# Gated recurrence of a two-layer trunk: half of the tokens reversed, one product per level over packed keys, the diagonal by a product with ones

## Chip, cores and metric

The kernel runs on one core of a Trainium2 chip. The metric is the device time of one execution in microseconds. Before the change it is 628.70 us, the median of three runs (628.10 to 628.72). The engines are called as in the profile: PE is TensorE, DVE is VectorE, ACT is ScalarE, POOL is GpSimd, SP issues most DMAs.

## What is computed

A trunk of two layers over 256 tokens of 1024 features in float32. Layer 0 mixes tokens by a gated linear recurrence with 8 heads of 128 features, layer 1 by causal attention with a table of relative positions. A feed-forward part follows each.

```python
def hgrn2_mixer(h, w_in, w_out, lb, out_norm):
    # S_t = diag(f_t) S_{t-1} + (1 - f_t) i_t^T ; o_t = S_t^T q_t, per head
    q, fz, inp, og = jnp.split(h @ w_in, ...)
    q = silu(q)
    f = lbf + (1.0 - lbf) * sigmoid(fz)
    k = 1.0 - f
    ...
    o = rms_norm(o, out_norm) * sigmoid(og)
    return o @ w_out

def reference(x, ...):
    for layer in range(2):
        y = rms_norm(h, norm_mix[layer])
        y = hgrn2_mixer(y, ...) if layer == 0 else moba_mixer(y, ...)
        h = h + y
        h = h + swiglu(rms_norm(h, norm_ffn[layer]), ...)
    return rms_norm(h, final_norm)
```

In closed form, the score of query t on key s (s not after t) is the sum over the 128 features n of q[t,n] k[s,n] f[s+1,n] ... f[t,n], and the output is the sum of scores times the input i.

## The kernel before

**The stream of products.** Each weight is split into a rounded part and a rest, whi and wlo, both in a rounded 32-bit format, and each activation into xh and xl (hh and hl in the feed-forward part). A weight tile of 128 x 128 is used in three *main products* with 256 columns: whi with xh, wlo with xh, whi with xl (`mm_w`, all issued in L478). The weights come as blocks of 128 x 1024 by DMA from SP into `raw`; ACT writes whi (L435), DVE writes wlo (L437). The ring of whi and wlo holds six blocks, and a new whi waits until PE has done with the block six places earlier.

**The recurrence of a head** works on q and k with features on the partitions and the 256 tokens along the free axis, as two halves of 128 tokens. The products of the gates are taken by levels m = 1, 2, 4, ..., 64. At level m the tokens lie in pairs of blocks of m, and queries of the late block meet keys of the early block; the weights between them are products of gates. `forget` (L815) makes f, k and, on POOL, the gate products tot of blocks of 2, 4, ..., 64 (L831). `query` (L834) makes q. `step` (L858) goes from level m to 2m: it multiplies half of q and half of k by tot on DVE (L865, L867) and copies the other halves on ACT (L869, L872) into new tiles Q[2m], K[2m].

`scores` (L896) issues the products. The first (L919, tile mov) has 192 columns for each half: the diagonal, which uses k and silu(q) before any gate, and level 1. The levels 2, 4, 8, 16 (L913) have 64 columns for each half, so two products a level. Level 32 and level 64 share two products of 128 columns (L940), because ACT has joined them (L879, L881), and the *far* product of half 1's queries on half 0's keys has 128 (L942). All these operands are float32. DVE copies what a mask admits from PSUM into the score tile pm (L907, L924), ACT copies level 32, 64 and far (L950 to L954). Two value products of pm with ii follow (L961, L962), then `result` (L966) makes the next split activations.

**Order.** The class `Order` decides it while the program is built: each operation has an engine, a cost, a due time and the buffers it waits for. Between main products the scheduler places what it takes for ready by its costs; products of the recurrence are placed 1.5 us (by its clock) after their operands are ready. Each engine then runs its queue strictly in that order. The projections of two heads (`EARLY_HEADS`) run at the opening together with the token-wide projection; six heads follow, three projections of 24 main products each, and then the output projection w_out with 192 main products, in which the norm over all heads (sto: sums, power on POOL, transposes L621, row rrow on ACT) is finished. `residual` (L626) multiplies by that row on DVE (yt), adds (hT) and makes the xh (ACT, L565) and xl (DVE) of the first feed-forward layer.

**The table** of attention (L1010 to L1026): a product of 384 columns (L1019), one DMA to DRAM and eight DMAs back from POOL that skew it into bt. The logits read it in L1162.

Of the kernel before, what the change touches and what calls it, by code (L numbers as in the profile page):

```python
# [15 lines left out]
P = 128  # L16
S = 256
# [12 lines left out]
LEVELS = (1, 2, 4, 8, 16)  # L30
# [295 lines left out]
def hybrid_trunk(ctx: ExitStack, tc: tile.TileContext, wts, xT, par, gfin, tab, onehot, masks, out):  # L326
# [14 lines left out]

    def new(tag, shape, bufs=1, dt=FT, held=False):
        return ring(tag, shape, bufs, dt).new(held)
# [204 lines left out]
    bt = new("bt", [P, NH * S])  # L548
    bt.tile = bt.ring.make()
    mk = fixed("mk", [P, NMK], U8)  # L550
    oh = fixed("oh", [33, 384])
# [3 lines left out]
    def tables():  # L555
        od.op("S", 60, lambda: nc.sync.dma_start(mk.tile, masks), writes=[mk], nbytes=NMK * P, due=65)
        od.op("S", 60, lambda: nc.sync.dma_start(oh.tile, onehot), writes=[oh], nbytes=60000, due=100)
# [244 lines left out]

    class Core:
# [3 lines left out]
        def __init__(self, h):  # L807
            self.h = h
            self.f = new("ff", [P, S], 2)
            self.so = new("so", [P, S], 3)  # L810
            self.Q = {m: new(f"q{m}", [P, S], 2) for m in (1, 2, 4, 8, 16, 32, 64)}
            self.K = {m: new(f"k{m}", [P, S], 2) for m in (1, 2, 4, 8, 16, 32, 64)}
            self.tot = {1: self.f}

        def forget(self, b):  # L815
# [6 lines left out]
            k1 = self.K[1]  # L822
            od.op("A", ca(S), lambda: A.activation(k1.tile, f.tile, AF.Identity, scale=-1.0, bias=1.0), reads=[f],
                  alloc=[k1], due=7)
            for m in (1, 2, 4, 8, 16, 32):
# [6 lines left out]
                od.op("G", cg(S // (2 * m)), prod, reads=[a], alloc=[t], due=8)  # L832

        def query(self, b):  # L834
            f, q1 = self.f, self.Q[1]
            b, src = normed(self.h, b, 6)
            sg = new("sgq", [P, S], 3)
            self.mov = mov = new("mov", [P, 2, 192], 2)
            two = lambda t: t.rearrange("p (a t) -> p a t", a=2)
            od.op("A", ca(S), lambda: A.activation(sg.tile, src(), AF.Sigmoid), reads=[b], alloc=[sg], due=6)  # L840
            od.op("V", cv(S), lambda: V.tensor_tensor(mov[:, :, :P], two(src()), two(sg.tile), op=OP.mult),
                  reads=[b, sg], alloc=[mov], due=6)
            od.op("V", cv(S), lambda: V.tensor_tensor(two(q1.tile), mov[:, :, :P], two(f.tile), op=OP.mult),
                  reads=[mov, f], alloc=[q1], due=7)
            od.op("A", ca(P), lambda: A.activation(
                mov[:, :, P:], q1.tile.rearrange("p (a t z) -> p a t z", a=2, z=2)[:, :, :, 1], AF.Copy),
                reads=[q1], writes=[mov], due=8)
# [10 lines left out]
        def step(self, m, due):  # L858
            Q, K, tot = self.Q, self.K, self.tot[m]
            nb = S // (2 * m)  # L860
            if m < 64:
                q, qn, k, kn = Q[m], Q[2 * m], K[m], K[2 * m]
                v4 = lambda t: t.tile.rearrange("p (b z m) -> p b z m", z=2, m=m)
                bc = lambda z: tot.tile.rearrange("p (b z) -> p b z", z=2)[:, :, z:z + 1].to_broadcast([P, nb, m])
                od.op("V", cv(P), lambda: V.tensor_tensor(v4(qn)[:, :, 1], v4(q)[:, :, 1], bc(0), op=OP.mult),  # L865
                      reads=[q, tot], alloc=[qn], due=due)
                od.op("V", cv(P), lambda: V.tensor_tensor(v4(kn)[:, :, 0], v4(k)[:, :, 0], bc(1), op=OP.mult),  # L867
                      reads=[k, tot], alloc=[kn], due=due)
                o = od.op("A", ca(P), lambda: A.activation(v4(qn)[:, :, 0], v4(q)[:, :, 0], AF.Copy), reads=[q],  # L869
                          writes=[qn], due=due + .1)  # L870
                o.deps.append(qn.writers[0])
                o = od.op("A", ca(P), lambda: A.activation(v4(kn)[:, :, 1], v4(k)[:, :, 1], AF.Copy), reads=[k],  # L872
                          writes=[kn], due=due + .1)
                o.deps.append(kn.writers[0])
                if m == 32:


                    v2 = lambda t: t.tile.rearrange("p (a x) -> p a x", a=2)
                    od.op("A", ca(64), lambda: A.activation(v2(k)[:, :, 96:128], v2(kn)[:, :, 0:32], AF.Copy), reads=[kn],  # L879
                          writes=[k], due=due + .2)  # L880
                    od.op("A", ca(P), lambda: A.activation(  # L881
                        q.tile.rearrange("p (a y z x) -> p a y z x", a=2, y=2, z=2)[:, :, :, 0],
                        v2(qn)[:, :, 64:128].rearrange("p a (y x) -> p a y x", y=2), AF.Copy), reads=[qn], writes=[q],
                        due=due + .2)
                return
            self.q128, self.k128 = q, k = new("q128", [P, P], 2), new("k128", [P, P], 2)
            Q, K = Q[64], K[64]

            def last():
                A.activation(q[:, 64:], Q[:, 192:], AF.Copy, scale=tot[:, 2:3])  # L890
                A.activation(q[:, :64], Q[:, P:192], AF.Copy)
                A.activation(k[:, :64], K[:, :64], AF.Copy, scale=tot[:, 1:2])
                A.activation(k[:, 64:], K[:, 64:P], AF.Copy)
            od.op("A", 4 * ca(64) + 186, last, reads=[Q, K, tot], alloc=[q, k], due=due)

        def scores(self, due):  # L896
            h, Q, K, mov = self.h, self.Q, self.K, self.mov
# [3 lines left out]
            def take(b, c, m, stride=64):  # L901
                dst = pm.tile.rearrange("p a (b z m) -> p a b z m", z=2, m=m)
                src = b[:, c:c + 2 * stride].rearrange("p (a x) -> p a x", a=2)[:, :, stride - 64:]
                src = src.rearrange("p a (b m) -> p a b m", m=m)
                msk = mk[:, moff[m]:moff[m] + P].rearrange("p (a b m) -> p a b m", a=2, m=m)
                r = P - m
                V.copy_predicated(dst[:r, 0:3:2, :, 1], msk[:r], src[:r])  # L907
# [12 lines left out]
            od.op("T", 2 * ct(192), s0, reads=[K[1], mov], alloc=[b0], due=due)  # L920

            def s0e():
                v = b0[:, :384].rearrange("p (a x) -> p a x", a=2)
                V.copy_predicated(pm[:, 0:3:2, :], mk[:, :2 * P].rearrange("p (a x) -> p a x", a=2), v[:, :, :P])  # L924
            od.op("V", cv(S), s0e, reads=[b0, mk], writes=[pm], due=due)
            od.op("V", cv(P), lambda: take(b0, 0, 1, 192), reads=[b0, mk], writes=[pm], due=due)
            for m in (2, 8):
                b = bank("A")
                o1 = od.op("T", 2 * ct(64), lambda b=b, m=m: level(b, 0, m), reads=[K[m], Q[m]], alloc=[b], due=due)
# [443 lines left out]
```

## Time and profile before

| | us |
|---|---|
| median of the runs | 628.70 |
| profiled execution | 627.57 |
| its span, first to last instruction | 625.8 |
| opening and first two heads' projections | 0 to about 46 |
| recurrence, eight heads | about 46 to 136 |
| rest of the output projection | to 149 |
| first feed-forward layer | 149 to about 326 |

The profile gives for each group of instructions a line of the program, an engine, output and inputs by name, shapes, a count, busy time and mean duration, and for idle time the instruction that ended it. Timeline rows begin with the start in us from the span's start and the duration. Recorded matmul durations overlap, so PE's steps are read from start to start. "x4" at the end of a timeline row joins four records.

### The profile page before, as it was taken

How to read it: one execution, taken by the hardware profiler on the slowest of the kernel's cores; microseconds unless marked ns; L12 is line 12 of the kernel's file. 1: busy time of each engine (PE TensorE's matmuls, PEld its weight loads, DVE VectorE, ACT ScalarE, POOL GpSimd, SP SyncE). 2: the span in 40 equal slices, each digit the busy share in tenths (PEclk: the TensorE clock that was granted, in tenths of full speed). 3: DMA queues.
4: the chain of work that ended last, by engine and by line, in shares of the span. 5: the costliest groups of instructions: out<-in, count | busy, mean ns of one | idle time of the engine just before them, and what ended most of it. 6: DMA issues, size and time to landing. Idle time of an engine off the chain costs nothing.

```text
span 625.8 us, 12443 instructions
## 1 busy us (share of the span) xinstructions
PE 615.6 (98%) x4848; PEld 592.8 (95%) x4848; DVE 443.1 (71%) x803; ACT 363.4 (58%) x715; POOL 36.7 (6%) x74
## 2 busy tenths in 40 slices
PE   8999999999999999999999999999999999999995
PEld 7899999999999999999998899999899999999994
DVE  6987989778686666666669678866676666666653
ACT  6779888857554444444447566565664444444443
POOL 0121112100300000000000000000100000000003
PEclk9999999999999999999999999999999999999999
DMA  8962534443996665666653665445645666556501
GB/s 315 331 208 93 179 103 169 132 139 106 236 282 197 201 187 193 195 198 191 189 198 121 215 206 169 139 162 172 202 160 178 203 202 200 184 182 181 163 2 67
DMA packets 31848, 111.83 MB, mean 179 GB/s; under 512 B 3804, under 2 KB 4221, under 8 KB 31789
## 3 DMA queue, kind: packets, MB, share of 16 engines
q1 hardware_dynamic: 30764, 108.71, 53.5%
q0 software_dynamic: 448, 1.25, 1.0%
q10 hardware_dynamic: 576, 1.08, 0.5%
q8 instruction: 38, 0.62, 0.4%
q14 instruction: 22, 0.17, 0.1%
HBM read 109.78 MB, written 1.25 MB: 177 GB/s over the span
## 4 chain that ended last, share of the span: by engine, by line
PE 79%; issue 16%; DVE 3%; DMA 1%; ACT 1%; POOL 1%; SPq 0%; ACTq 0%; DVEq 0%; POOLq 0%
PE psB L478 42%; PE psA L478 36%; DVE wlo L437 1%; DMA raw<-in_w_dram 1%; POOL ny L617 1%; DVE xl L567 0%; DVE yt L632 0%; DVE hT L634 0%; DVE sqacc L585 0%; PE psB L1228 0%; ACT whi L435 0%; PE psA L621 0%; DVE raw L1259 0%; ACT sq L1262 0%; ACT raw L1289 0%
## 5 line engine op out<-in xcount | busy, mean ns | idle before, releaser
L437 DVE TENSOR_TENSOR wlo<-raw,whi 128x1024 fp32r<-128x1024 f32 (+1 forms) x206 | 248.1, 1214 | 110.5 <-ACT whi L435 110.1
L435 ACT ACTIVATE whi<-raw 128x1024 fp32r<-128x1024 f32 (+1 forms) x205 | 213.0, 1050 | 149.0 <-issue 69.9
L478 PE MATMUL psA<-xh,whi 128*128 128x256 f32 x592 | 163.5, 279 | 0.0
L478 PE MATMUL psA<-xh,wlo 128*128 128x256 f32 x592 | 161.8, 277 | 0.0
L478 PE MATMUL psB<-xh,whi 128*128 128x256 f32 x560 | 157.9, 286 | 0.0
L478 PE MATMUL psA<-xl,whi 128*128 128x256 f32 x592 | 157.1, 277 | 0.0
L478 PE MATMUL psB<-xh,wlo 128*128 128x256 f32 x560 | 154.1, 279 | 0.0
L478 PE MATMUL psB<-xl,whi 128*128 128x256 f32 x560 | 149.9, 279 | 0.0
L478 PEld LDWEIGHTS psA<-xh,whi 128*128 128x128 f32 x592 | 111.2, 188 | 0.8 <-issue 0.5
L478 PEld LDWEIGHTS psA<-xh,wlo 128*128 128x128 f32 x592 | 111.3, 188 | 0.3
L478 PEld LDWEIGHTS psA<-xl,whi 128*128 128x128 f32 x592 | 108.2, 188 | 0.0
L478 PEld LDWEIGHTS psB<-xh,wlo 128*128 128x128 f32 x560 | 105.6, 189 | 0.7
L478 PEld LDWEIGHTS psB<-xh,whi 128*128 128x128 f32 x560 | 105.4, 188 | 0.8
L478 PEld LDWEIGHTS psB<-xl,whi 128*128 128x128 f32 x560 | 103.0, 189 | 0.0
L478 PE MATMUL psB<-hl,whi 128*128 128x256 f32 x176 | 48.7, 277 | 0.0
L478 PE MATMUL psB<-hh,whi 128*128 128x256 f32 x176 | 48.7, 277 | 0.0
L478 PE MATMUL psB<-hh,wlo 128*128 128x256 f32 x176 | 48.7, 276 | 0.0
L1039 ACT ACTIVATE u<-sgq 128x256 f32<-128x256 f32 x44 | 18.0, 410 | 38.9 <-DVE sgq L1037 38.7
L478 PE MATMUL psA<-wlo,hh 128*128 128x512 f32 x88 | 34.6, 393 | 0.0
L478 PE MATMUL psA<-whi,hl 128*128 128x512 f32 x88 | 34.5, 392 | 0.0
L478 PE MATMUL psA<-whi,hh 128*128 128x512 f32 x88 | 34.5, 392 | 0.0
L478 PEld LDWEIGHTS psB<-hl,whi 128*128 128x128 f32 x176 | 33.1, 188 | 0.0
(178 smaller groups left out, 789.6 us busy)
## 6 DMA issues: line engine op xcount, KB each, us to landing
raw<-in_w_dram SPq DMA_DIRECT2D x202, 512.0 KB, 4.2
raw<-in_w_dram SPq DMA_DIRECT2D x4, 256.0 KB, 5.0
bt<-scr POOLq DMA_DIRECT2D x8, 128.0 KB, 8.3
hT<-in_x_dram SPq DMA_DIRECT2D x1, 512.0 KB, 6.1
bt<-in_final_dram ACTq DMA_DIRECT2D x1, 512.0 KB, 4.9
out_dram<-raw ACTq DMA_DIRECT2D x2, 256.0 KB, 2.3
out_dram<-raw SPq DMA_DIRECT2D x2, 256.0 KB, 2.0
hT<-in_x_dram SPq DMA_DIRECT2D x2, 128.0 KB, 5.0
```

Source lines behind the costliest of these rows:

```text
L435: od.op("A", ca(n), lambda h=h, r=r, o=o, n=n: A.activation(h[:, :n], r[:, o:o + n], AF.Copy), reads=[r], alloc=[h], due=due)
L437: od.op("V", cv(n), lambda h=h, lo=lo, r=r, o=o, n=n: V.tensor_tensor(lo[:, :n], r[:, o:o + n], h[:, :n].bitcast(FT), op=OP.subtract), rea ...
L478: T.matmul(o, a, b, start=start, stop=stop, skip_group_check=True)
L617: od.op("G", 500, lambda: G.tensor_tensor(y.tile, v.tile, mhalf, op=OP.pow), reads=[v], alloc=[y], due=due)
L1039: od.op("A", ca(S), lambda: A.activation(sg.tile, gs.tile, AF.Sigmoid), reads=[gs], alloc=[sg], due=due)
```

## The change

**Tokens 128 to 255 come in reverse order** (and go out in it; the host undoes it). In half 1 the early block of a pair is now the second one. So the early keys of both halves, put at their own positions, fill 128 columns without overlap, and likewise the late queries take 64 columns for each half. A level tile E[m] holds 128 key columns and 128 query columns, and **one product of 128 x 128** serves both halves; what it forms across halves the masks leave out. Level 32 is treated as the others, level 64 has its own product.

**q and k stay in place.** `step` first copies the early keys and the late queries into E[m] on ACT, then multiplies those parts of k and q by tot in place on DVE.

**The diagonal** is q times k per token, summed over features. POOL forms the product `own`, ACT rounds it (eh), POOL forms the rest (el), and two products with a matrix of ones, with rounded operands and 256 columns, give the sums in every row; a mask keeps the diagonal. The ones are written by ACT with a due time of 20 tiles.

**The scheduler** counts POOL's gate products as 120 + 6.6 n instead of 150 + 2.1 n (ns, n outputs).

**The table** gets a mirrored part for reversed queries: 512 columns instead of 384, sixteen DMAs of 128 or 256 columns a row instead of eight of 256, three blocks of 128 a head in bt.

```diff
-LEVELS = (1, 2, 4, 8, 16)
+LEVELS = (1, 2, 4, 8, 16, 32)
+    def picked(t, m, late):
+        return walk(t, m if late else 0, [P - m if late else P + m, 2], [2 * m, 64 // m], [1, m])
+    allone = fixed("allone", [P, P], FR)
+    od.op("A", ca(P), lambda: A.activation(allone.tile, ident, AF.Copy, scale=0.0, bias=1.0), writes=[allone], due=20)
...
-                od.op("G", cg(S // (2 * m)), prod, reads=[a], alloc=[t], due=8)
+                od.op("G", 120 + 6.6 * (S // (2 * m)), prod, reads=[a], alloc=[t], due=8)
...
+            od.op("G", 830, lambda: G.tensor_tensor(own[0].tile, sg.tile, k1.tile, op=OP.mult), reads=[sg, k1],
+                  alloc=[own[0]], due=18)
+            od.op("A", ca(S), lambda: A.activation(own[1].tile, own[0].tile, AF.Copy), reads=[own[0]], alloc=[own[1]], due=20)
+            od.op("G", 1040, lambda: G.tensor_tensor(own[2].tile, own[0].tile, own[1].tile.bitcast(FT), op=OP.subtract),
+                  reads=own[:2], alloc=[own[2]], due=22)
...
+            late, early = (lambda: picked(q.tile, m, 1)), (lambda: picked(k.tile, m, 0))
+            od.op("A", ca(P), lambda: A.activation(keys(), early(), AF.Copy), reads=[k], alloc=[e], due=due)
+            o = od.op("A", ca(P), lambda: A.activation(flat(P), late(), AF.Copy), reads=[q], writes=[e], due=due)
             if m < 64:
+                od.op("V", cv(P), lambda: V.tensor_tensor(early(), early(), by(1), op=OP.mult),
+                      reads=[k, tot], writes=[k], due=due)
+                od.op("V", cv(P), lambda: V.tensor_tensor(late(), late(), by(0), op=OP.mult),
+                      reads=[q, tot], writes=[q], due=due)
...
             def level(b, c, m):
-                o = Q[m].tile.rearrange("p (a b z m) -> p a b z m", a=2, z=2, m=m)[:, :, :, 1]
-                for a in range(2):
-                    mm(b[:P - m, c + 64 * a:c + 64 * a + 64], K[m][:, a * P:a * P + P - m], o[:, a], start=True, stop=True)
+                mm(b[:, c:c + P], E[m][:, :P], E[m][:, P:], start=True, stop=True)
...
             def s0():
-                for a in range(2):
-                    mm(b0[:, 192 * a:192 * a + 192], K[1][:, a * P:a * P + P], mov[:, a], start=(a == 0), stop=True)
+                for i in (1, 2):
+                    mm(b0[:, :S], allone.tile, own[i].tile, start=(i == 1), stop=(i == 2))
...
             def far():
-                A.activation(pm[0:32, 0:3:2, 32:64], v[0:32, :, 32:64], AF.Copy)
-                A.activation(pm[64:96, 0:3:2, 96:128], v[64:96, :, 96:128], AF.Copy)
-                A.activation(to[32:64], w[32:64], AF.Copy)
-                A.activation(to[0:32], w[96:128], AF.Copy)
-                A.activation(pm[:, 1, :], b3[:, 2 * P:3 * P], AF.Copy)
+                A.activation(pm[0:64, 0, 64:], b3[0:64, :64], AF.Copy)
+                A.activation(pm[64:, 2, :64], b3[64:, 64:P], AF.Copy)
+                A.activation(pm[:, 1, :], b3[:, P:2 * P], AF.Copy)
...
-    od.op("T", ct(384), lambda: mm(eb[:, :384], tbr.tile, oh.tile, start=True, stop=True), reads=[tbr, oh], alloc=[eb], due=80)
+    od.op("T", ct(512), lambda: mm(eb[:, :], tbr.tile, oh.tile, start=True, stop=True), reads=[tbr, oh], alloc=[eb], due=80)
     for a in range(P // REP):
+        for c0, n, at, step in ((0, P, REP * a, 1), (P, S, S - 1 - REP * a, -1)):
+            od.op("G", 1000, lambda a=a, c0=c0, n=n, at=at, step=step: G.dma_start(
...
+    order = np.r_[:P, S - 1:P - 1:-1]
+    xT = np.ascontiguousarray(a["x"][0][order].T.reshape(KT, P, S).transpose(1, 0, 2))
```

**Where it moves instructions.** PE's queue before, in the projections of the last head: the far product (q_1730), the diagonal with level 1 (mov, two products), level 2 (two products) between main products.

```order
L478 MATMUL psA<-q_1730,k_1731 128x128
L478 MATMUL psA<-mov,k_1706 128x192 x2
L478 MATMUL psA<-q_1782,k_1749 126x64 x2
L478 MATMUL psB<-xh_448,whi 128x256
L478 MATMUL psB<-xh_448,wlo 128x256
L478 MATMUL psB<-xl_455,whi 128x256
```

PE's queue after, near the same place: value products (pm), one level (q_1713), the diagonal (eh and el on the ones), main products, another level (q_1760).

```order
L487 MATMUL psA<-pm_558,ii 128x256
L487 MATMUL psA<-pm_558,ii 128x128
L487 MATMUL psA<-q_1713 128x128
L487 MATMUL psA<-eh,allone 128x256
L487 MATMUL psA<-el,allone 128x256
L487 MATMUL psB<-xh_530,whi 128x256
L487 MATMUL psB<-xh_530,wlo 128x256
L487 MATMUL psB<-xl_538,whi 128x256
L487 MATMUL psB<-xh_391,whi 128x256
L487 MATMUL psB<-xh_391,wlo 128x256
L487 MATMUL psB<-xl_403,whi 128x256
L487 MATMUL psA<-q_1760 128x128
```

A level is one product instead of two, and the diagonal's pair stands by itself. It stands 81 main products behind the end of the head's q projection for the first of the six later heads and 39 for the last.

ACT's queue at the end of the recurrence, before: square and xh of the last head, two weight blocks, the norm's row, two weight blocks, the first xh of the feed-forward layer.

```order
L594 ACTIVATE sq<-psA 128x256
L975 ACTIVATE xh_2218<-u 128x256
L435 ACTIVATE whi<-raw 128x1024 x2
L624 ACTIVATE rrow<-psA 128x256
L435 ACTIVATE whi<-raw 128x1024 x2
L565 ACTIVATE xh_2349<-hT,pv 128x256
```

The same place after:

```order
L605 ACTIVATE sq<-psA 128x256
L967 ACTIVATE xh_2224<-u 128x256
L444 ACTIVATE whi<-raw 128x1024 x2
L635 ACTIVATE rrow<-psA 128x256
L1008 ACTIVATE tbr<-tb 33x128
L576 ACTIVATE xh_2318<-hT,pv 128x256
```

Counted from the start of the program, the last weight block ahead of the feed-forward layer's first xh is the same in both (the 47th); it now stands ahead of rrow. On PE the last head's value products stand 66 main products ahead of the feed-forward layer (102 before), the norm's sums 33 (75 before), the transposes 15 (57 before).

DVE's queue at that place, before:

```order
L606 TENSOR_TENSOR sqacc<-sqacc 128x256
L437 TENSOR_TENSOR wlo<-raw,whi 128x1024
L614 TENSOR_SCALAR nv<-psA 128x2
L437 TENSOR_TENSOR wlo<-raw,whi 128x1024 x2
L632 TENSOR_TENSOR yt<-psB,rrow 128x512 x2
L634 TENSOR_TENSOR hT<-yt,hT 128x512 x2
```

And after:

```order
L617 TENSOR_TENSOR sqacc<-sqacc 128x256
L446 TENSOR_TENSOR wlo<-raw,whi 128x1024
L625 TENSOR_SCALAR nv<-psA 128x2
L446 TENSOR_TENSOR wlo<-raw,whi 128x1024
L643 TENSOR_TENSOR yt<-psB,rrow 128x512 x2
L645 TENSOR_TENSOR hT<-yt,hT 128x512 x2
```

The split ahead of yt is that of the block after the one that stood there before.

More of the change, by code (lines that the diff above doesn't have):

```diff
@@ L810, in __init__ @@
             self.so = new("so", [P, S], 3)
-            self.Q = {m: new(f"q{m}", [P, S], 2) for m in (1, 2, 4, 8, 16, 32, 64)}
-            self.K = {m: new(f"k{m}", [P, S], 2) for m in (1, 2, 4, 8, 16, 32, 64)}
+            self.E = {m: new(f"q{m}", [P, S], 2) for m in (1, 2, 4, 8, 16, 32, 64)}
+            self.k, self.q, e, self.far, eh, el = (new(f"k{i}", [P, S], 2) for i in (1, 2, 4, 8, 16, 32))
+            self.own = [e, rings["eh"].new(), rings["el"].new()]
             self.tot = {1: self.f}
@@ L887, in step @@
-            Q, K = Q[64], K[64]
+            w = self.far
             def last():
[L890 to L894, printed above, removed]
+                A.activation(w[:, :64], k[:, :64], AF.Copy, scale=tot[:, 1:2])
+                A.activation(w[:, 64:P], k[:, 64:P], AF.Copy)
+                A.activation(w[:, P:192], q[:, P:192], AF.Copy, scale=tot[:, 3:4])
+                A.activation(w[:, 192:], q[:, 192:], AF.Copy)
@@ L896, in scores, with take @@
+            od.op("A", 4 * ca(64) + 186, last, reads=[q, k, tot], alloc=[w], due=due)
         def scores(self, due):
-            h, Q, K, mov = self.h, self.Q, self.K, self.mov
+            h, E, own, w = self.h, self.E, self.own, self.far
             pm = pms[h % 2]
             moff = {m: 2 * P + P * i for i, m in enumerate(LEVELS)}
[L901 to L907, printed above, removed]
+            def take(b, c, m):
+                dst = walk(pm.tile.rearrange("p a t -> p (a t)"), m, [2 * P - m, 2], [2 * m, 64 // m], [1, m])
+                shape = lambda t: t.rearrange("p (a b x) -> p a b x", a=2, x=m)
+                V.copy_predicated(dst, shape(mk[:, moff[m]:moff[m] + P]), shape(b[:, c:c + P]))
@@ L925, in scores @@
             od.op("V", cv(S), s0e, reads=[b0, mk], writes=[pm], due=due)
[L926 to L929, printed above, removed]
-                o2 = od.op("T", 2 * ct(64), lambda b=b, m=m: level(b, P, 2 * m), reads=[K[2 * m], Q[2 * m]], writes=[b],
-                           due=due)
-                o2.deps.append(o1)
-                for i in range(2):
-                    od.op("V", cv(P), lambda b=b, m=m, i=i: take(b, P * i, m << i), reads=[b, mk], writes=[pm], due=due)
@@ L935, in scores @@
-            b3 = bank("A")
-            def both():
-                for a in range(2):
-                    c = slice(a * P, a * P + P)
-                    mm(b3[:, c], K[32][:, c], Q[32][:, c], start=True, stop=True)
-            o2 = od.op("T", 2 * ct(P), both, reads=[K[32], Q[32]], alloc=[b3], due=due)
-            o3 = od.op("T", ct(P), lambda: mm(b3[:, 2 * P:3 * P], self.k128.tile, self.q128.tile, start=True, stop=True),
-                       reads=[self.k128, self.q128], writes=[b3], due=due)
+            b, c = b0, S
@@ new lines, in scores @@
+            for m in LEVELS:
+                if c == 4 * P or m == 16:
+                    b, c, last = bank("A"), 0, None
+                o = od.op("T", 220, lambda b=b, c=c, m=m: level(b, c, m), reads=[E[m]], due=due,
+                          **(dict(writes=[b]) if last else dict(alloc=[b])))
+                if last:
+                    o.deps.append(last)
+                last = o
+                od.op("V", cv(P), lambda b=b, c=c, m=m: take(b, c, m), reads=[b, mk], writes=[pm], due=due)
+                c += P
@@ L1010, in hybrid_trunk @@
     REP = 16
-    scr = dr.tile([P, 384], FT, name="scr")
+    scr = dr.tile([P, 512], FT, name="scr")
     scr_b = Buf(None)
-    e = new("be", [P, 384])
+    e = rings["lg"].new()
     eb = bank("B")
@@ L1215, in hybrid_trunk @@
     st3.finish("A", 40)
-    gf = new("bt", [P, NH * S])
+    gf = new("bt", None)
     gf.tile = bt.tile[:, :D]
@@ L1330, in _constants @@
     import numpy as np
-    onehot = np.zeros((33, 384), np.float32)
-    for i in range(384):
-        dist = 255 - i
+    onehot = np.zeros((33, 512), np.float32)
+    for i in range(512):
+        dist = 255 - i if i < S else i - 383
         if dist < 0:
```

106 lines of the change are left out of this document (46 added, 60 removed).

## The prediction

> **What bounds the kernel now.** The page comes first: where the span goes, and which engine ends last.
>
> ```profile
> span 625.8 us, 12443 instructions
> PE 615.6 (98%) x4848; PEld 592.8 (95%) x4848; DVE 443.1 (71%) x803; ACT 363.4 (58%) x715; POOL 36.7 (6%) x74
> PE 79%; issue 16%; DVE 3%; DMA 1%; ACT 1%; POOL 1%; SPq 0%; ACTq 0%; DVEq 0%; POOLq 0%
> ```
>
> TensorE (PE) is busy for 98% of the span and carries 79% of the chain that ended last. Whether it waits for anyone is told by the list of waits of PE, which is complete here:
>
> ```profile
> PE psA L478 <- POOL ident masks.py:199: 1.4, 1, 1.4
> PE psA L478 <- DVE sqacc L606: 0.8, 1, 0.8
> PE psA L621 <- POOL ny L617: 0.4, 1, 0.4
> PE psB L478 <- DVE wlo L437: 0.2, 1, 0.2
> ```
>
> All its waits come to 2.8 us. None is for the recurrence's own work: L606 and L617 are the sums of a norm. So the kernel is one queue of products that hardly pauses, and a product taken out of the recurrence is worth its whole step on PE, as long as no new wait takes its place. The windows of the recurrence (58 to 140 us), of what follows it, and of the first feed-forward layer say how much room the other engines have (length; then busy time of PE, PE's weight loads, DVE, ACT, POOL):
>
> ```profile
> 58.00:140.00 82.00, 82.00 (x694) 81.56 (x693) 67.57 (x163) 67.93 (x217) 13.39 (x36) 1.00 0.45 149
> 166.00:320.00 154.00, 154.00 (x1359) 154.00 (x1358) 101.36 (x143) 73.51 (x100) 0.00 (x0) 1.00 0.65 206
> ```
>
> In the recurrence DVE and ACT are both busy for 82 to 83%, far above the 66% and 48% later. That is where a shorter PE queue can run into them.
>
> **What a product costs.** Recorded durations of matmuls overlap, so I count from start to start in PE's timeline. A product of float32 operands appears as two records ("x4" is two products).
>
> ```profile
> 81.19 0.28 PE L478 MATMUL psB<-xl,whi 128*128 128x256 f32 x1
> 81.32 0.51 PE L478 MATMUL psA<-q,k 128*112 128x64 f32 x4
> 81.64 0.36 PE L478 MATMUL psB<-xh,whi 128*128 128x256 f32 x1
> 81.84 0.28 PE L478 MATMUL psB<-xh,wlo 128*128 128x256 f32 x1
> ...
> 82.32 0.28 PE L478 MATMUL psB<-xl,whi 128*128 128x256 f32 x1
> 82.43 0.60 PE L478 MATMUL psA<-q,k 128*128 128x128 f32 x4
> 83.00 0.28 PE L478 MATMUL psB<-xh,wlo 128*128 128x256 f32 x1
> ...
> 122.16 0.28 PE L478 MATMUL psB<-xl,whi 128*128 128x256 f32 x1
> 122.28 0.81 PE L478 MATMUL psA<-mov,k 128*128 128x192 f32 x4
> 123.05 0.28 PE L478 MATMUL psB<-xh,wlo 128*128 128x256 f32 x1
> ...
> 142.16 0.38 PE L621 MATMUL psA<-ident,ny 128*128 128x128 f32 x2
> 142.50 0.28 PE L478 MATMUL psB<-xh,wlo 128*128 128x256 f32 x1
> ...
> 149.09 0.28 PE L478 MATMUL psA<-xh,whi 128*128 128x256 f32 x1
> ```
>
> The main step first: 56 main products start between 142.50 and 149.09, 0.118 us each. The first main record behind a float32 block starts early and the second makes up for it (81.64 to 81.84 is 0.20), so a block's cost runs from the last main record ahead of it to the second behind it, less two steps (0.236). The level of 64 columns, two products: 81.84 - 81.19 - 0.236 = 0.414 us. Two products of 128 columns: 83.00 - 82.32 - 0.236 = 0.444, so 0.222 each. The diagonal with level 1 in it, two products of 192 columns: 123.05 - 122.16 - 0.236 = 0.654. Half the columns save next to nothing: 0.104 us a record at 64 columns, 0.111 at 128. A record here costs what its weights cost, and the change halves the number of weight loads of a level.
>
> [...]
>
> **The change, part by part.**
>
> *PE in the recurrence.* Before, a head has 0.654 (diagonal and level 1), four levels at 0.414 (1.656; 2, 4, 8 and 16 have the same shape but for a few weight columns), two products at level 32 (0.444) and the far one (0.222): 2.976. After: two products of rounded operands with 256 columns, which have the shape of a main product (0.236), seven levels and the far one at 0.222 each (1.776): 2.012. The value products stay. That is 0.964 us a head and **7.7 us** for eight.
>
> *The table's product* moves 512 columns instead of 384.
>
> ```profile
> 153.26 0.84 PE psB L478 x2
> ```
>
> By columns 0.84 becomes 1.12: **+0.3** (bounds 0 and 0.3).
>
> *DVE, ACT, POOL in the recurrence.* DVE gains one masked copy a head. ACT loses the copy into mov, two joins of level 32 and two of five far copies, and gains two level copies and the 256-wide eh, so it stays level. POOL gains two 256-wide products a head, which no row shows. The nearest rows are 128 wide and 512 wide, alone and beside a split:
>
> ```profile
> 91.58 2.35 DVE L437 TENSOR_TENSOR wlo<-raw,whi 128x1024 fp32r<-128x1024 f32 x2
> 92.88 1.31 POOL L831 TENSOR_TENSOR tot<-ff 128x128 f32<-128x128 f32 x1 [11.51 <-ACT ff L820]
> 116.87 0.40 POOL L831 TENSOR_TENSOR tot<-ff 128x128 f32<-128x128 f32 x1 [9.73 <-DVE pm L907]
> L1264 POOL TENSOR_TENSOR raw<-raw,bt 128x512 f32<-128x512 f32 x4 | 5.3, 1328 | 171.5 <-DVE raw L1259 171.5
> L907 DVE COPY_PREDICATED pm<-mk,psA 112x128 f32<-112x128 uint8 x1 | 0.3, 301 | 0.0
> 104.61 0.58 POOL L831 TENSOR_TENSOR tot<-ff 128x128 f32<-128x128 f32 x1 [8.74 <-ACT ff L820]
> 104.85 0.62 DVE L976 TENSOR_TENSOR xl<-u,xh 128x256 fp32r<-128x256 f32 x1
> 138.15 0.42 DVE L976 TENSOR_TENSOR xl<-u,xh 128x256 fp32r<-128x256 f32 x1
> ```
>
> The same POOL product takes 0.40 us alone and 1.31 when it meets a split (91.58 to 93.93): it waits the split out. DVE pays too: the 256-wide xl takes 0.62 beside a POOL product (104.61), against 0.42 without one (138.15). By columns between 0.40 and 1.33, a new POOL product takes 0.70 alone, and up to 0.9 more behind a split. For DVE I bound the blocking of each by 0 and 0.7 and take 0.2, by the xl row: 0.4 a head. With the copy (0.3) DVE has 0.7 more in each head. Seven heads' worth in the window turn 67.6 busy of 82.0 into 72.5 of 75.3. That is full, but busy time counts the tail of each record, which the next one overlaps (two splits at 91.58 take 2.35, one at 144.73, quoted below, takes 1.22), so the queue still fits. **I take no wait**; the upper bound is a rival below.
>
> The Trainium skill, "SBUF — State Buffer", section "Who interferes with whom", calls the port pair of VectorE and GpSimd an exclusive lock that a VectorE instruction with two SBUF inputs takes too. The 1.31 beside 0.40 agrees; by it DVE would lose the whole 0.70 twice a head, and the 72.5 above would be 79.5 of 75.3.
>
> *The end of the recurrence.* In the new order the row of norm factors comes late: between its transposes (L621) and the first feed-forward product stand 15 main products, where 57 stood. And two weight blocks that stood behind that row on ACT stand ahead of it; on DVE the split of the second stands ahead of yt. How long the chain takes is in these rows of before:
>
> ```profile
> 143.64 1.06 ACT L435 ACTIVATE whi<-raw 128x1024 fp32r<-128x1024 f32 x1 [0.68 <-PE psB L478]
> 144.73 1.22 DVE L437 TENSOR_TENSOR wlo<-raw,whi 128x1024 fp32r<-128x1024 f32 x1 [1.82 <-ACT whi L435]
> 145.88 1.28 DVE L632 TENSOR_TENSOR yt<-psB,rrow 128x512 f32<-128x512 f32 x2
> 146.47 1.06 ACT L435 ACTIVATE whi<-raw 128x1024 fp32r<-128x1024 f32 x1 [1.77 <-PE psB L478]
> 147.79 0.91 ACT L565 ACTIVATE xh<-hT,pv 128x256 fp32r<-128x256 f32 x2 [0.27 <-DVE hT L634]
> ```
>
> The whi at 146.47 waits for PE to free its buffer. From there PE has 149.09 - 146.47 = 2.62 us of main products to the feed-forward layer, and 0.22 for the transposes that now lie in between: 2.84. After the change this same block stands ahead of rrow on ACT, and its wlo ahead of yt on DVE. So the chain from its start is whi to wlo 1.09, wlo to yt 1.15, yt to xh 1.91 (two yt and one hT, in the same order), xh about 0.5: 4.65. PE waits **1.8 us** at the first feed-forward product. Bounds: 0, if the block's buffer comes free early enough, and 3, if head 7 is a wlo (1.2) late. From there on the order is that of before, but for one or two places.
>
> *Costs put at nothing.* The ones are made on ACT ahead of the first whi, where it idles for 2.6 us. Uncovered they would cost 0.3. The table's eight more DMAs hold POOL for 4.3 us:
>
> ```profile
> 6.57 1.29 ACT L435 ACTIVATE whi<-raw 128x512 fp32r<-128x512 f32 x2 [2.60 <-DMA raw<-in_w_dram]
> 157.72 2.15 POOL L1023 DMA_DIRECT2D bt<-scr  x4 [2.03 <-DMA scr<-be]
> 161.29 1.63 POOL L617 TENSOR_TENSOR ny<-nv,mhalf 128x2 f32<-128x2 f32 x1 [1.43 <-DVE nv L614]
> ```
>
> The next norm's ny now stands behind six of them instead of four, 1.1 us more, and it idled 1.43 there. Their 0.5 MB more lie beside weight loads that run ahead: whi waits for buffers, not for data, in the rows above. The logits read as many table columns as before.
>
> *Sum.* The profiled execution took 627.57 us (span 625.8). 627.57 - 7.7 + 0.3 + 1.8 = 622.0. The median of the runs is 628.70, 1.1 above that execution, so I forecast **623.1**.
>
> **The rivals.**
>
> 1. *No new wait at the end* (the yt gets ahead, or the buffer frees early): 623.1 - 1.8 = 621.3. For it: no wait of this kind in before. Against: the fixed order of whi and rrow. 15%.
> 2. *DVE and POOL block each other*, and level products come late by 0.2 to 0.45 us in each head: +1.6 to +3.6, so 624.7 to 626.7. For it: 72.5 of 75.3. Against: no level was waited for so far. 17%.
> 3. *Slower: the diagonal waits for POOL.* Its two products now hang on sigmoid, DVE, POOL, ACT, POOL, and in PE's queue everything stands behind them. If both POOL products wait a split out (1.31 - 0.40 = 0.9 each) and nothing covers it, a head loses 1.8: 623.1 + 14.4 = 637.5. It decides from 0.7 us a head, (628.7 - 623.1) / 8. Against: the diagonal stands 39 (last head) to 81 main products behind the end of its projection, 4.6 to 9.6 us; the chain without queues is about 0.4 + 0.4 + 0.7 + 0.4 + 0.7 = 2.6. 6%.
> 4. *PE's pace shifts.* The main step is 154/1359 = 0.113 us in the feed-forward layer and 0.118 around 145 us, with no wait in either. If a different stream puts the layer at 0.118, it costs 1359 x 0.0047 = 6.4: 629.5. Nothing in the profile says what sets it. 5%.
> 5. *The levels are not cheaper*: a record goes by its columns after all, 0.056 at 64. Then the four levels cost 0.89 a head instead of 1.66 before, and 1.6 us is gained in all: 629.2. The rows above speak plainly against it. 2%.
>
> **How the numbers follow.** The forecast has 55%. A measurement of this kernel tells 0.2% from no change, that is 627.4 to 630.0. Faster: forecast, 1 and 2, 87%. Within 0.2%: 4 and 5, 7%. Slower: 3, 6%. The range reaches from rival 1 with a little more from the levels (0.4 less each than I took would be 0.440 a pair: 0.8 in all), 620.4, to the far end of rival 2, 626.7; with the unknown 1.2 us at the end already inside it, I set 620.3 to 626.9.
>
> **What would show it.** In the changed profile a level's x2 costs 0.22 from start to start, the pair of ones products 0.24, and the same stretch of work ends about 7.7 us of PE time sooner. PE's list of waits gains one of about 1.8 us on xh at the first feed-forward product. POOL's 256-wide products take 0.7, some 1.6. If PE waits for el, q or pm inside the recurrence, rival 2 or 3 holds; if PE's records of the feed-forward layer show 0.118, rival 4; if nothing waits at its start, rival 1.

## The result and the profile after

| | us |
|---|---|
| before, median of five runs | 628.10 |
| after, median of five runs (630.86 to 635.71) | 632.68 |
| ratio after to before | 1.0082, 95% interval 1.0059 to 1.0104 |
| profiled execution after, its span | 632.68, 630.9 |

The change makes the kernel slower by 0.8%. The page of the changed kernel, the same three lines as before (span; busy time by engine; the chain that ended last):

```profile
span 630.9 us, 12211 instructions
PE 614.9 (97%) x4784; PEld 589.1 (93%) x4784; DVE 450.2 (71%) x811; ACT 363.0 (58%) x700; POOL 57.7 (9%) x98
PE 64%; issue 17%; DVE 12%; ACT 5%; DMA 1%; POOL 1%; SPq 0%; DVEq 0%; ACTq 0%; POOLq 0%
```

PE's busy time hardly moved, though it has fewer products: three level products take 1.28 us in a row quoted below, where three at 71.09 us take 0.98, so a record can include time in which it waits. The line to read is the chain: PE gave up 15 points, and VectorE rose from 3% to 12%. The list of PE's waits, complete, says where (engine waited for; us in total, times, longest):

```profile
PE psA L487 <- DVE pm L909: 2.5, 5, 1.0
PE psA L487 <- DVE hT L645: 1.8, 1, 1.8
PE psA L487 <- POOL ident masks.py:199: 1.4, 1, 1.4
PE psA L487 <- DVE pm L924: 0.7, 2, 0.4
PE psA L487 <- DVE sqacc L617: 0.6, 1, 0.6
PE psA L632 <- POOL ny L628: 0.5, 1, 0.5
PE psA L487 <- ACT q L883: 0.5, 1, 0.5
PE psB L487 <- DVE wlo L446: 0.4, 1, 0.4
```

Those on pm and q are new and lie in the recurrence, 3.7 us in all; the one on hT is the wait at the first feed-forward product. The windows of the recurrence and of the feed-forward layer, with the columns of before (length; busy PE, weight loads, DVE, ACT, POOL; clock), and below them a shorter window of the recurrence, first before, then after:

```profile
58.00:140.00 82.00, 77.83 (x630) 74.91 (x629) 75.22 (x172) 65.93 (x201) 26.20 (x42) 1.00 0.48 155
166.00:320.00 154.00, 154.00 (x1357) 154.00 (x1357) 100.89 (x142) 74.06 (x100) 6.86 (x11) 1.00 0.65 202
```

```profile
58.00:115.00 57.00, 57.00 (x481) 56.69 (x481) 48.85 (x123) 49.51 (x162) 11.62 (x30) 1.00 0.48 158
```

```profile
58.00:115.00 57.00, 53.22 (x427) 50.85 (x426) 54.63 (x123) 47.20 (x143) 22.82 (x34) 1.00 0.50 159
```

From 58 to 115 us VectorE went from 48.9 to 54.6 busy of 57.0 for the same 123 records: it is full, and PE is no longer. GpSimd's busy time doubled. The 123 records are longer, not more. (A full VectorE alone does not hold PE: in experiment 10 it is 54.8 busy of 57.0 in this window, but with 142 records, and PE is 56.7 busy.) The groups of VectorE's products with the gate totals from 40 to 146 us, before and then after (x40: count; busy time, mean ns; idle time before them):

```profile
L865 DVE TENSOR_TENSOR q<-q,tot 128x128 f32<-128x128 f32 x40 | 12.0, 300 | 3.6 <-ACT q L869 2.7 <-issue 0.8
L867 DVE TENSOR_TENSOR k<-k,tot 128x128 f32<-128x128 f32 x40 | 11.5, 288 | 0.0
```

```profile
L889 DVE TENSOR_TENSOR k<-k,tot 128x128 f32<-128x128 f32 x40 | 15.2, 379 | 2.3 <-ACT q L883 2.2
L887 DVE TENSOR_TENSOR k<-k,tot 128x128 f32<-128x128 f32 x40 | 12.4, 311 | 1.6 <-ACT q L882 1.5
```

What one such meeting looks like is in the timeline of the changed kernel, where rows begin with start and duration:

```profile
72.38 1.22 DVE L446 TENSOR_TENSOR wlo<-raw,whi 128x1024 fp32r<-128x1024 f32 x1
...
72.61 1.58 POOL L860 TENSOR_TENSOR k<-sgq,k 128x256 f32<-128x256 f32 x1 [1.99 <-ACT whi L444]
...
73.51 0.83 DVE L889 TENSOR_TENSOR k<-k,tot 128x128 f32<-128x128 f32 x1
...
74.27 1.22 DVE L909 COPY_PREDICATED pm<-mk,psA 128x128 f32<-128x128 uint8 x3
...
74.75 1.28 PE L487 MATMUL psA<-q 128*128 128x128 f32 x6 [0.55 <-DVE pm L909]
```

GpSimd's product starts inside a split and ends at 74.19, after 1.58 us; the shortest one of its kind takes 0.73. VectorE's next product with two operands in SBUF takes 0.83 where the plain ones take 0.28, and ends 0.15 behind GpSimd's. The masked copies stand behind it, and PE's level products wait for a copy to free their bank.

**Where the 5.1 us between the two spans arise.** Main products are the same in both kernels and stand in the same order, so the start of the same main product in the two timelines tells how far one kernel is ahead. I number the 4440 records from 0; product 840 lies behind all score and value products of the recurrence, product 864 is the first of the feed-forward layer. After minus before, in us:

| main product | 120 | 360 | 480 | 600 | 840 | 960 | 2640 | 3360 | 4320 |
|---|---|---|---|---|---|---|---|---|---|
| start before | 27.0 | 70.0 | 90.1 | 109.4 | 146.3 | 161.7 | 365.4 | 462.1 | 596.2 |
| after minus before | 0.11 | -4.31 | -2.81 | -1.52 | 0.06 | 4.17 | 4.17 | 5.12 | 5.12 |

The gain is there at first, is lost again through the recurrence, then 4.1 us are lost at one place, the start of the feed-forward layer, and 0.95 in attention.

### The profile page after: what moved, and what is told of

Read it like the earlier page. It is cut to its first block, busy times and chain, and to the rows that moved or that the text cites. A ratio compares the mean times of both kernels' runs of the same rounds, so it can differ in the third digit from the quotient of the medians.

```text
span 630.9 us, 12211 instructions
## 1 busy us (share of the span) xinstructions
PE 614.9 (97%) x4784; PEld 589.1 (93%) x4784; DVE 450.2 (71%) x811; ACT 363.0 (58%) x700; POOL 57.7 (9%) x98
## 3 DMA queue, kind: packets, MB, share of 16 engines
q0 software_dynamic: 720, 1.84, 1.6%
## 4 chain that ended last, share of the span: by engine, by line
PE 64%; issue 17%; DVE 12%; ACT 5%; DMA 1%; POOL 1%; SPq 0%; DVEq 0%; ACTq 0%; POOLq 0%
PE psA L487 32%; PE psB L487 32%; DVE wlo L446 4%; DVE k L889 1%; DVE pm L909 1%; ACT whi L444 1%; DVE k L887 1%; DMA raw<-in_w_dram 1%; ACT q L882 1%; ACT q L883 1%; DVE yt L643 1%; POOL ny L628 1%; DVE hT L645 0%; DVE xl L578 0%; DVE k L858 0%
## 5 line engine op out<-in xcount | busy, mean ns | idle before, releaser
L628 POOL TENSOR_TENSOR ny<-nv,mhalf 128x2 f32<-128x2 f32 x5 | 7.6, 1511 | 317.5 <-DVE nv L625 317.5
```

What stands on the lines that cost most here:

```text
L628: od.op("G", 500, lambda: G.tensor_tensor(y.tile, v.tile, mhalf, op=OP.pow), reads=[v], alloc=[y], due=due)
```

## The experiments

Three theories for the recurrence. **Theory 1**: GpSimd's two own products per head hold VectorE's SBUF products back, VectorE is full, and level products come late. **Theory 2**: the high parts of the weights come late on ScalarE at 40 to 59 us, and the splits in arrears crowd VectorE. **Theory 3**: the order that the scheduler wrote with GpSimd's new durations is bad. For the start of the feed-forward layer, a separate question: what makes the wait, and what follows it. "Product 840" below is the row of the table above. Kernels of one group ran on one chip beside the kernel before, whose medians were 628.25, 628.91, 628.80 and 628.18.

| kernel | median | ratio to before, 95% | product 840 | product 960 |
|---|---|---|---|---|
| after | 632.68 | 1.0082 (1.0059 to 1.0104) | 0.06 | 4.17 |
| e1_memset | 627.39 | 0.9991 (0.9971 to 1.0010) | -5.42 | -1.29 |
| e2_before_pool | 630.62 | 1.0037 (1.0024 to 1.0050) | 2.31 | 2.32 |
| e3_diag_pe | 623.63 | 0.9929 (0.9912 to 0.9947) | -5.22 | -5.75 |
| e4_tail_dummy | 631.30 | 1.0055 (1.0040 to 1.0070) | 0.05 | 2.39 |
| e5_old_pool_cost | 629.77 | 1.0018 (1.0006 to 1.0029) | -2.99 | 0.84 |
| e6_diag_pe_old_cost | 623.75 | 0.9920 (0.9904 to 0.9937) | -5.65 | -6.18 |
| e7_half_dose | 629.09 | 1.0015 (0.9990 to 1.0039) | -3.65 | 1.75 |
| e8_quarter_pieces | 631.79 | 1.0045 (1.0028 to 1.0062) | -0.77 | 3.33 |
| e9_last_head_pe | 628.90 | 1.0002 (0.9991 to 1.0012) | 0.47 | -0.06 |
| e10_two_heads_pool | 622.62 | 0.9903 (0.9888 to 0.9917) | -5.50 | -6.03 |

**1. GpSimd writes only.**

```diff
-G.tensor_tensor(own[0].tile, sg.tile, k1.tile, op=OP.mult)
+G.memset(own[0].tile, 0.5)
...
-G.tensor_tensor(own[2].tile, own[0].tile, own[1].tile.bitcast(FT), op=OP.subtract)
+G.memset(own[2].tile.bitcast(FT), 0.0)
```

> The changed kernel with GpSimd's two own 128x256 products per head replaced by fills of the same tiles at the same places in the same order (leaves out the diagonal of the scores). Theory 1 (the two products hold back VectorE, whose SBUF-SBUF products stretched from 286 to 381 ns a record in the recurrence; its 8.1 us of excess makes the level products late): the k<-k,tot record falls back below 300 ns, VectorE's excess to about 2 us, the time to 624 to 627. Theory 2 (the weights' high parts come late on ScalarE at 40 to 59 us, and the splits in arrears crowd VectorE) and theory 3 (the order that the scheduler wrote is bad): ScalarE's work and the order are as they were, so 631 to 633.

Measured: 627.39, and 5.5 us of the lead stay at product 840 (-5.42 against 0.06), with the order of every engine as in the changed kernel. VectorE's groups are back at the durations of before:

```profile
L889 DVE TENSOR_TENSOR k<-k,tot 128x128 f32<-128x128 f32 x40 | 12.1, 302 | 2.6 <-ACT q L883 2.5
L887 DVE TENSOR_TENSOR k<-k,tot 128x128 f32<-128x128 f32 x40 | 11.6, 289 | 1.7 <-ACT q L882 1.3 <-issue 0.3
```

The fills take 311 ns each, and the two groups are within 0.1 us of those of before. The median is 0.4 above the range that theory 1 gave, since the wait at the feed-forward layer and what follows it (4.1 us from product 840 to 960, as in the changed kernel) are still there. Theory 2 alone and theory 3 alone are excluded: ScalarE's work and the order were the same. Six groups of VectorE products with both operands in SBUF (those with totals or gates, and the split xl) take 41.2 us in the changed kernel and 35.5 here: GpSimd's 16 products cost VectorE 5.7 us, 0.36 each, and PE 5.5 us.

**2. The two products added to the kernel before.**

```diff
                     G.tensor_tensor(t.tile, v[:, :, 0], v[:, :, 1], op=OP.mult)
+                    if m == 32:
+                        G.tensor_tensor(dm[0].tile, f.tile, k1.tile, op=OP.mult)
+                        G.tensor_tensor(dm[1].tile, dm[0].tile, f.tile, op=OP.subtract)
```

> The kernel before with two more GpSimd products of 128x256 per head, from f and k into a scratch tile that nothing reads, behind the last total. Theory 1: VectorE's excess in the recurrence rises from 1.9 us towards 8; VectorE was 86% busy there, so part of it is hidden: time 630 to 634 against 628.1. Theories 2 and 3: VectorE's records stay near 290 ns or the stretch is hidden, 627.9 to 629.

630.62, as theory 1 expected: slower by 0.37%, with the order of every other instruction as before. Price in a kernel that had room on VectorE: 2.3 us at product 840, 0.3 a head.

**3. The diagonal on TensorE, the rest of the change kept.**

```diff
-G.tensor_tensor(own[0].tile, sg.tile, k1.tile, op=OP.mult)
-A.activation(own[1].tile, own[0].tile, AF.Copy)
-G.tensor_tensor(own[2].tile, own[0].tile, own[1].tile.bitcast(FT), op=OP.subtract)
+A.activation(own[0].tile, k1.tile, AF.Copy)
...
-for i in (1, 2):
-    mm(b0[:, :S], allone.tile, own[i].tile, start=(i == 1), stop=(i == 2))
+for a in range(2):
+    c = slice(a * P, a * P + P)
+    mm(b0[:, c], own[0][:, c], sg[:, c], start=(a == 0), stop=True)
```

> The changed kernel with the diagonal from TensorE again: two float32 products of 128 columns per head (k kept in a copy by ScalarE, silu(q) as the moving operand) in place of GpSimd's two products and the two 256-column sums by ones. TensorE +0.21 us per head, 1.7 in all; GpSimd's 14.6 us of own products are gone, ScalarE has as many copies as before it. Theory 1: 632.7 + 1.7 - 6 to 8 = 626 to 629. Theories 2 and 3: 632.7 + 1.7, 633 to 635.

623.63, better than any theory said, and faster than the kernel before by 0.7%. By the prices of the prediction TensorE has 1.7 us more to do than in the changed kernel, and the time is 9.0 less. The expectation missed that the wait at the feed-forward layer would go too: its list of waits has no entry on hT.

**4. TensorE kept busy during the wait at the feed-forward layer.**

```diff
     od.written(sto.row)
+    db = main_bank("A")
+    for _ in range(10):
+        mm(db[:, :P], ident, ident, start=True, stop=True)
+    db.held = False
     swiglu(0, x1, st1, "A", down0)
```

> The changed kernel with ten float32 products of ident by ident (128 columns, 2.2 us) put in front of the first product of the feed-forward layer, where TensorE waits 1.8 us for the last normalized rows. If that wait is what brings the granted clock of 0.5 for 3.4 us behind it: the stretch at half clock is gone, the main products behind it are 0.118 us apart again, and the time falls by 1.5 to 2, to about 631. If the half clock has another cause: it stays, and the time is 632 to 633.

631.30, 1.4 less. The windows behind the wait, first of the changed kernel, then of this one (the number behind POOL's is the granted clock):

```profile
150.00:154.00 4.00, 2.71 (x13) 1.82 (x14) 4.00 (x9) 3.27 (x8) 0.00 (x0) 0.96 0.37 122
154.00:158.00 4.00, 4.00 (x24) 4.00 (x24) 4.00 (x8) 3.12 (x5) 1.52 (x3) 0.61 0.19 70
```

```profile
150.00:154.00 4.00, 4.00 (x29) 3.10 (x28) 4.00 (x9) 3.28 (x8) 0.00 (x0) 1.00 0.38 126
154.00:158.00 4.00, 4.00 (x37) 4.00 (x37) 4.00 (x8) 3.18 (x5) 1.70 (x3) 1.00 0.17 66
```

The clock of 0.61 is gone, 37 records stand where 24 stood, and 1.8 us are won from product 840 to 960 (4.11 against 2.34), though the first feed-forward product starts no sooner. So the pause cost its own 2.0 us, and the half clock behind it 1.8.

**5 and 6. The scheduler's durations for GpSimd undone**, in the changed kernel and in that of experiment 3.

```diff
-od.op("G", 120 + 6.6 * (S // (2 * m)), prod, reads=[a], alloc=[t], due=8)
+od.op("G", cg(S // (2 * m)), prod, reads=[a], alloc=[t], due=8)
...
-od.op("G", 830, lambda: G.tensor_tensor(own[0]
+od.op("G", cg(S), lambda: G.tensor_tensor(own[0]
...
-od.op("G", 1040, lambda: G.tensor_tensor(own[2]
+od.op("G", cg(S), lambda: G.tensor_tensor(own[2]
```

> The changed kernel with the old GpSimd durations in the scheduler (150 + 2.1 ns an element for the totals, 688 for each own product in place of 830 and 1040); the work is the same, the order moves. Theory 3 (the order that the new durations wrote costs the time): 627 or less, or more than 635. Theory 1 (GpSimd's reading products hold VectorE wherever they stand): the k<-k,tot records stay at 360 to 390 ns and the time within 631 to 634.

> The kernel with the diagonal on TensorE (623.63) with the old GpSimd durations for the totals. It tells what the new durations are worth without GpSimd's own products. Theory 1: they matter little, 623 to 625. Theory 3: 621 or less, or 626 and more.

629.77: neither expectation holds. With GpSimd's products in place the order is worth 2.9 us in the medians (4.0 by the ratios to the kernel before) and 3.05 at product 840, so theory 3 has a share. The products with the totals fell too, from 27.6 us to 26.0 in all:

```profile
L887 DVE TENSOR_TENSOR k<-k,tot 128x128 f32<-128x128 f32 x40 | 13.5, 339 | 1.2 <-ACT q L882 1.1
L889 DVE TENSOR_TENSOR k<-k,tot 128x128 f32<-128x128 f32 x40 | 12.5, 315 | 1.0 <-ACT q L883 0.4
```

Without GpSimd's own products the same edit is worth nothing (623.75 against 623.63), as theory 1 expected. So the order matters through where GpSimd's products fall; which placement decides was not tried.

**7. One real product, one fill.**

```diff
-G.tensor_tensor(own[2].tile, own[0].tile, own[1].tile.bitcast(FT), op=OP.subtract)
+G.memset(own[2].tile.bitcast(FT), 0.0)
```

> The changed kernel with GpSimd's first own product real and its subtraction replaced by a fill (the low part is zero: leaves out the diagonal's low half). Theory 1: half of the 5.3 us between the changed kernel and the one with both filled comes back, 629.5 to 631, k<-k,tot at about 340 ns. Rival: only one of the two products hurts, the subtraction that runs beside the levels (then near 627.4) or the first (then near 632.7).

629.09, a little below the range; but the ten runs spread from 626.86 to 633.50, so product 840 tells more. There the profiled execution reads 0.06, -3.65, -5.42 for two, one and no real product: the second product (the subtraction, which runs beside the levels) costs 3.7 and the first 1.8. Both hurt, the subtraction more.

**8. The products in quarters.**

```diff
-G.tensor_tensor(own[0].tile, sg.tile, k1.tile, op=OP.mult)
+[G.tensor_tensor(own[0][:, c:c + 64], sg[:, c:c + 64], k1[:, c:c + 64], op=OP.mult)
+ for c in range(0, S, 64)]
...
-G.tensor_tensor(own[2].tile, own[0].tile, own[1].tile.bitcast(FT), op=OP.subtract)
+[G.tensor_tensor(own[2][:, c:c + 64], own[0][:, c:c + 64],
+                 own[1][:, c:c + 64].bitcast(FT), op=OP.subtract) for c in range(0, S, 64)]
```

> The changed kernel with each own product cut into four of 64 columns, the same elements and places. If VectorE is held for the length of one GpSimd instruction: the longest k<-k,tot record falls from 0.84 us to below 0.5, the sum of the stretch is about the same or larger by the fixed part of more instructions, and the time is 631 to 635. If what holds VectorE is only the start of an instruction: stretch and time rise, 635 or more. If a long instruction alone holds it: below 629.

631.79, within the first case. The longest product with a total is 0.49 us (0.84 in the changed kernel), as for a hold that lasts one GpSimd instruction. The sum of the two groups fell too, from 27.6 to 25.6 us, which was not expected. GpSimd pays for it: 64 columns take 449 and 443 ns, so an own product takes 1.8 us instead of 0.8 to 1.0, and PE now waits for el too (1.2 us in two waits). Little is won.

**9. The last head alone on TensorE.**

```diff
+self.direct = self.h == NH - 1
...
+if self.direct:
+    A.activation(own[0].tile, k1.tile, AF.Copy)
+else:
+    ...
```

> The changed kernel with the diagonal of the last head alone on TensorE (two float32 products, +0.21 us), the other seven by GpSimd and ones. In the order the two turns of the output norm now stand some 40 main products ahead of the feed-forward layer, where the changed kernel has 16 and the kernel before 58. If the wait at the first feed-forward product comes from the last head's longer way through GpSimd, ScalarE and GpSimd: that wait of 1.8 us and the half clock behind it are gone, about 3.5 less and 0.6 less of VectorE's stretch: 628 to 630 against 632.7. If it comes from the shorter levels alone: the wait stays, 631.5 to 633.

628.90. At product 840 it stands at 0.47, no better than the changed kernel's 0.06: the 0.6 expected there did not come, so GpSimd's products of the last head cost PE nothing that shows. Nothing is lost at the feed-forward layer either: -0.06 at product 960, where the changed kernel has 4.17. So the wait hung on the last head's way through GpSimd, ScalarE and GpSimd again, which put the norm's turns 15 main products ahead of the feed-forward layer; here they stand some 40 ahead.

**10. Heads 0 and 1 through GpSimd, the others on TensorE** (the edit of 9 with `self.h > 1`).

> The diagonal of heads 0 and 1 by GpSimd and ones, of heads 2 to 7 on TensorE. TensorE -0.42 us against the kernel with all eight on TensorE (623.63). Theory 1 prices GpSimd's two products at 0.66 us a head of lost time (5.3 over 8): 623.2 + 1.3 = 624 to 625. If the stretch of the first two heads is hidden, because VectorE is 78% busy at 40 to 58 us: 623.0 to 623.4.

622.62: theory 1's even price per head is wrong here, and the second case holds, with 0.4 more than it gave. GpSimd's products of these two heads do hold VectorE (from 40 to 60 us the products with totals take 345 and 325 ns, in experiment 3 298 and 294), but it is busy for only 13.2 of 18.0 us from 40 to 58 us, and PE loses next to nothing.

```profile
58.00:140.00 82.00, 81.65 (x694) 80.93 (x693) 72.75 (x180) 69.47 (x206) 16.93 (x31) 1.00 0.52 168
```

In the window where the changed kernel had 77.8 of 82.0 on PE, this one has 81.7. It beats both kernels, so it was timed once more beside that of experiment 3 on one chip.

> Heads 0 and 1 by GpSimd and ones, 2 to 7 on TensorE, once more beside the next one on one chip. If VectorE has room for GpSimd's products at 40 to 58 us, this is faster than the next by the 0.42 us that TensorE saves, or a little more: 622.3 to 623.2. If the 1.0 us between the two medians was the difference of two chips: both within 0.3 of each other.

> All eight diagonals on TensorE once more, on the same chip as the one before it: 623.2 to 624.0; the ratio to the kernel before at 0.991 to 0.994.

622.66 (0.9902, 0.9882 to 0.9922) and 623.29 (0.9918, 0.9898 to 0.9938). The difference of 0.63 us is near the 0.42 that TensorE saves, but the intervals overlap, and the two profiled executions are only 0.13 us apart at product 840 (-5.53 and -5.40): that one is better than the other is not shown. Both are faster than the kernel before by 0.8 to 1%.

## Why the prediction was wrong

**TensorE's side of the sum was right.** The prediction gave 0.222 us to a product of 128 columns and 0.24 to the pair with ones. Of the changed kernel, two stretches of PE's timeline without a wait:

```profile
77.99 0.28 PE L487 MATMUL psB<-xh,wlo 128*128 128x256 f32 x1
78.11 0.28 PE L487 MATMUL psB<-xl,whi 128*128 128x256 f32 x1
78.22 0.28 PE L487 MATMUL psA<-eh,allone 128*128 128x256 f32 x1
78.34 0.28 PE L487 MATMUL psA<-el,allone 128*128 128x256 f32 x1
78.46 0.28 PE L487 MATMUL psB<-xh,whi 128*128 128x256 f32 x1
...
104.57 0.28 PE L487 MATMUL psB<-xl,whi 128*128 128x256 f32 x1
104.68 0.60 PE L487 MATMUL psA<-q 128*128 128x128 f32 x4
105.05 0.37 PE L487 MATMUL psB<-xh,whi 128*128 128x256 f32 x1
105.25 0.28 PE L487 MATMUL psB<-xh,wlo 128*128 128x256 f32 x1
```

The pair takes 78.46 - 78.22 = 0.24. Two levels take 105.25 - 104.57 - 0.236 = 0.444, one 0.222: rival 5 (levels not cheaper) falls. Where nothing holds VectorE, the saving arrives: the prediction's 7.7, less 1.7 for the diagonal on TensorE, is 6.0 for experiment 3. Summed by the prediction's own rule over the traces, all blocks between main products from product 120 to 840 cost 30.2 us before and 24.1 there, 6.1 less; its lead at product 840 is 5.2, as 0.3 was lost before product 120. In the changed kernel they cost 30.0 instead of the 22.5 that the prices give: the products were priced rightly, and the time went into waiting.

**The step that failed** is the one on DVE: "For DVE I bound the blocking of each by 0 and 0.7 and take 0.2, by the xl row", and on it "**I take no wait**". The xl row was one meeting of a short GpSimd product. In the changed kernel the meeting shown above costs a product with a total 0.55 (0.83 against 0.28), and over all 16 GpSimd products the hold is 0.36 each (experiment 1), 0.7 a head instead of 0.4. The larger error is the second half: the prediction compared sums over the window, found that the queue still fits, and concluded that nothing comes late. Of the 5.7 us that VectorE lost, 5.5 were lost by PE too. By the exclusive lock of "SBUF — State Buffer" ("Who interferes with whom") in the Trainium skill the prediction worked out the whole 0.70 for each product, 79.5 us of work in 75.3, and did not use it. The meeting shown agrees with that lock; as a price for every product 0.70 was too much, since not every product met one with two operands in SBUF.

**Rival 2 was the mechanism** (the two engines block each other and level products come late) with a price of 0.2 to 0.45 us a head. It measured about 0.7 by experiment 1, and about 1.0 by the whole gap at product 840 (7.7 expected, -0.06 got). These are averages: heads 0 and 1 (experiment 10) and the last one (experiment 9) cost next to nothing, so most of it seems to lie in the heads between them. The late levels stand in the list of what PE's weight loads wait for, which was empty before; from 40 to 150 us, the waits of the recurrence, first in the changed kernel, then in experiment 1:

```profile
PEld psA L487 <- DVE pm L909: 2.6, 5, 0.8
PEld psA L487 <- ACT q L883: 1.8, 2, 1.1
PEld psA L487 <- DVE pm L924: 1.0, 2, 0.6
PEld psA L487 <- ACT q L882: 0.3, 2, 0.2
```

```profile
PEld psA L487 <- DVE pm L909: 0.8, 2, 0.4
PEld psA L487 <- ACT q L883: 0.4, 1, 0.4
PEld psA L487 <- ACT q L882: 0.3, 2, 0.2
PEld psA L487 <- DVE pm L924: 0.2, 1, 0.2
```

So 1.7 us of the 2.3 that experiment 1 leaves open are late levels as well. Experiment 3 has the same 48 masked copies and none of these waits, so the copies alone do not make them; it has another order too, and which of the two decides was not tried. Of the loss, 3 us hang on the order that the new durations wrote (experiment 5), which the prediction did not count at all.

**Rival 3** crossed its threshold of 0.7 us a head, but not by its mechanism: no wait on eh or el is in the list. The levels and the copies were late, not the diagonal. **Rival 1** falls by the wait of 1.84 us below. **Rival 4** falls: the feed-forward window holds 1357 records in 154 us, before 1359.

**The tail wait was sized right and its consequence was missing.** "PE waits **1.8 us** at the first feed-forward product"; the changed kernel:

```profile
149.18 0.28 PE L487 MATMUL psB<-xl,whi 128*128 128x256 f32 x1
151.29 0.38 PE L487 MATMUL psA<-xh,whi 128*128 128x256 f32 x1 [1.84 <-DVE hT L645]
151.51 0.28 PE L487 MATMUL psA<-xh,wlo 128*128 128x256 f32 x1
151.72 1.12 PE L487 MATMUL psB<-oh,tbr 33*128 33x512 f32 x2
```

1.84, and the record of the table's product is 1.12, as worked out; from start to start it takes 1.05, 0.2 more than before. What the sum lacked is the clock behind the pause: 1.8 us more (experiment 4). The prediction took the wait from the shorter levels and the order; experiment 9 shows that the order came from the last head's longer chain.

**The sum by terms**, on the profiled executions: predicted 622.0, measured 632.68, 10.7 apart. Of these 7.8 are the recurrence (-7.7 against +0.06), 2.0 the start of the feed-forward layer (4.1 against 1.8 and 0.3), 0.95 attention. Of the last, 0.45 arise between products 2640 and 2880 in the changed kernel and in all experiments on it, and 0.0 in experiment 2, which has the attention of before; the strided reading of the table in the logits is the only edit there, and it was not taken out by itself. The other 0.5 comes in small steps between products 2880 and 3360, where experiment 2, with the code of before, lost 1.05; so it is no mark of the change. The low end of the range does not come out of its own terms either (621.3 - 0.8 is 620.5, and 0.440 for 0.444 a pair is 0.1 us in eight heads, not 0.8); nothing hangs on it.

## What to carry to other kernels

An engine that is 85% busy has little room for a neighbour that holds it: price a moved operation by what it does to the engines beside it before calling its engine free. That a window's sums still fit does not mean that nothing comes late: here 5.7 us more on VectorE became 5.5 on TensorE. GpSimd's reading products are cheap where VectorE has slack (heads 0 and 1) and cost more than the TensorE time that they replace where it has none (0.7 us a head on average against 0.2). In this kernel a pause of 2 us on TensorE cost its length and 1.8 us of slower clock behind it, so it is worth filling, or better, worth moving the work that causes it.

## What the runs showed of the hardware

Behind a pause of 2.0 us TensorE's granted clock fell to 0.5 for 3.4 us (0.61 in the window of 154 to 158 us), 2.4 us after it had started again, and dummy products in the pause kept it at 1.00. The profiles of the four experiments that had the same wait of 1.8 us (1, 5, 7 and 8) show such a fall too, 1.0 to 2.0 us after the restart, in experiment 7 for 6.8 us; the others (2, 3, 6, 9 and 10) show none before the last 7 us of the program, where every trace has one. A wait of 1.4 us in experiment 5, at 442 us, had none behind it. The five runs of the changed kernel spread with the mean clock: 630.86 at 0.997, 632.42 and 632.68 at 0.995, 634.41 at 0.993, 635.71 at 0.989. Since one fall costs 1.8 us, these would be none, one, two and about three falls of 3.4 us, as an estimate. And a GpSimd fill of 128x256 takes 311 ns and leaves VectorE's products with totals at 289 to 302 ns, while GpSimd products that read SBUF bring them to 311 to 379 ns and are themselves held by a split (0.73 at the shortest, 1.65 beside one).
